# Staggered addresses for the gathered tokens and the SwiGLU product in an expert layer

## The chip, the cores and the metric

The kernel runs on one core of a Trainium2 chip, as one program. The metric is device time in microseconds (us). Before the change three runs took 1880.63, 1880.92 and 1881.67 us; the median is 1880.92 us.

## What is computed

The reference is a backbone of two layers over 256 latent tokens and 256 context tokens of width 1024. Layer 0 has attention and spatial gating, then a dense SwiGLU. Layer 1 has latent attention, and then the part that the change touches: each latent token goes to its two best of eight experts.

```python
def moe_swiglu(h, w_router, b_router, w_gate, w_up, w_down):
    ...
    y = jnp.zeros_like(h)
    for e in range(N_EXPERTS):                       # 8
        y = y + combine[..., e:e + 1] * swiglu(h, w_gate[e], w_up[e], w_down[e])
    return y

def swiglu(h, w_gate, w_up, w_down):                 # 1024 x 3584, 1024 x 3584, 3584 x 1024
    return (jax.nn.silu(h @ w_gate) * (h @ w_up)) @ w_down
```

All data are float32. The kernel gets float32 accuracy out of a faster multiplication by splitting both factors into a high and a low part and adding three products (high·high, high·low, low·high): the helper `mm3`, L213 to L216.

## The kernel before

**The stream of weights.** All weights come from memory in blocks of 128 x 2048 numbers (1 MB), in one fixed order, by transfers that SyncE issues (`load`, L157). Each block is split (`split`, L165): ScalarE writes the high part `wh` (L177), VectorE writes the low part `wl` (L178). There are three buffers of each. TensorE reads them, and when it is done with a buffer the next split may write it.

**The experts (L1129 to L1154).** For each of 8 experts `e` the tokens that chose it, at most 128, are gathered by matmuls into the tile `xg` (`gather`, L978): for each of 8 slices `k` of the width it holds a high and a low block of 128 x 128, so 16 blocks of 512 bytes in each partition. There are two buffers of `xg`; the gathering for expert `e + 1` is done in small steps during expert `e`. The hidden width is done in 7 chunks `c` of 512 columns. For each chunk:

- `expert_in` (L1027): gate and up. For each of 8 slices, three matmuls with a block of `xg` as the stationary operand (128 x 128) and 512 columns of `wh` or `wl` as the moving operand: 24 matmuls for the gate, 24 for the up, into the PSUM tiles `mm`. VectorE multiplies the two into the tile `a` (L1035).
- `turn` (L1038): four transposes of `a`, and a split of the result into the tiles `ahi` and `alo` (128 x 512 each, four blocks of 512 bytes in each partition; two buffers of each).
- `expert_out` (L1046): down. 24 matmuls with blocks of `ahi` and `alo` as stationary operand and 512 columns of `wh` or `wl` as moving operand, into the PSUM tiles `pss`. They accumulate over the 7 chunks.

The turn and the down matmuls of a chunk come inside and behind the gate and up of the next chunk. When an expert is done its result is put back to the tokens by eight matmuls that read the tiles `yh`, `yl` and `ST` (`scatter_steps`, L1084); the last expert uses `scatter_now` and the tile `a` instead.

**Order and queues.** Each engine has its own queue and does its instructions in order. The framework chooses the order within a queue by simulated readiness and puts in the waits. TensorE runs matmuls and the loads of the stationary operand (PEld in the profile) side by side: while one matmul streams, the block for the next is loaded.

**Where the tiles lie.** Tiles of 128 partitions lie at one byte address in every partition. In the program of before these are the addresses that matter:

| tile | address | address mod 256 |
|---|---|---|
| wh, three buffers | 52384, 60576, 68768 | 160 |
| wl, three buffers | 76960, 85152, 93344 | 160 |
| xg, two buffers | 138656, 146848 | 160 |
| ahi, two buffers | 185280, 187328 | 192 |
| alo, two buffers | 189376, 191424 | 192 |
| ah of layer 0 (L214 to L216, moving operand) | 109984, 118176 | 160 |
| hx of layer 0 at its start (stationary operand there) | 166432 and three more, 8192 apart | 32 |

Every moving operand of 512 columns starts a whole number of 2048 bytes from the start of its tile, and every stationary block a whole number of 512 bytes, so the last column holds for each matmul.

The gains of the final norm lie in the tile `fg` (128 x 1024), loaded by two transfers of ScalarE's queue (L1141 to L1143) and read by VectorE after the last expert (L1165, L1196).

Of the kernel before, what the change touches and what calls it, by code (L numbers as in the profile page):

```python
# [8 lines left out]
F32 = mybir.dt.float32  # L9
F32R = mybir.dt.float32r  # L10
I32 = mybir.dt.int32
AF = mybir.ActivationFunctionType
ALU = mybir.AluOpType
# [3 lines left out]
P = 128  # L17
KD = 8
# [94 lines left out]
def _program(tc, A, out):  # L113
    nc = tc.nc
    act, vec, pe = nc.scalar, nc.vector, nc.tensor

    def newpool(name, bufs, side="left"):
        return tc.alloc_tile_pool(name=name, bufs=bufs, side=side, reuse_waits="tile")
# [11 lines left out]
    def nm(s):  # L130
        uid[0] += 1
        return f"{s}{uid[0]}"

    def ps_mm():
        return psp.tile([P, 512], F32, tag="mm", name=nm("mm"), bufs=4)

    def ps_s():
        return psp.tile([P, 512], F32, tag="s", name=nm("pss"), bufs=2)

    def ps_t():  # L140
        return psp.tile([P, 512], F32, tag="t", name=nm("pst"), bufs=2)
# [76 lines left out]
    def put_split(hi, lo, src):  # L218
        return (act.activation(hi, src, AF.Copy),
                vec.tensor_tensor(lo, src, hi.bitcast(F32), ALU.subtract))  # L220

# [1 line left out]
    def cload(key, shape, pool=const):  # L223
        t = pool.tile(shape, F32, tag=key, name="c_" + key)
        nc.scalar.dma_start(t, A[key])
        return t

    x = xp.tile([P, KD, T], F32, tag="x", name="x")
# [69 lines left out]
    def filler(n, get_ps):  # L298
        for _ in range(n):
            ada_unit(get_ps)  # L300
# [24 lines left out]
    def stats_begin(nk, nt):  # L325
        return {"nk": nk, "nt": nt, "acc": None, "ps": None}
# [59 lines left out]
            vec.scalar_tensor_tensor(x[:, db, a:b], ps[:, a:b], mod[:, l, g0 + db, c:c + 1], x[:, db, a:b],  # L386
                                     ALU.mult, ALU.add)

# [1 line left out]
    st = stats_begin(KD, 4)  # L390
    for k in range(KD):
        stats_add(st, x[:, k, :], k)
# [151 lines left out]
    proj_tok(2, ev_v)  # L544
    gp.release()

# [1 line left out]
    atp = newpool("atp", 2)  # L548
    first_out = where["evo", 0, 1]
    mixah, mixal = hx_pair()  # L550
# [70 lines left out]
    make_a(0, 1)  # L621
    

# [1 line left out]
    st = stats_begin(KD, 4)  # L625
    for cb in range(2):
        pss = [ps_mm() for _ in range(4)]
# [14 lines left out]
    make_a(1, 0)  # L642
    filler(4, ps_mm)

# [1 line left out]
    ffp = newpool("ffp", 2)  # L646
    bc = stats_end(st, 1024)
    hh, hl = hx_pair(), hx_pair()
# [65 lines left out]
    ffp.release()  # L714
    hxp.release()

# [1 line left out]
    filler(4, ps_mm)  # L718
    mlp = newpool("mlp", 1)
    mrp = newpool("mrp", 1, "right")  # L720
# [128 lines left out]
    mop1 = newpool("mop1", 1)  # L849
    tri, iota, ltm = mc[:, 0:128], mc[:, 128:256], mc[:, 256:320]  # L850
    wr, br = mc[:, 320:384].rearrange("p (k e) -> p k e", e=8), mc[:, 384:392]
    acc = mop1.tile([P, 2, 1024], F32, tag="acc", name="acc")
# [14 lines left out]
    for cb in range(2):  # L867
        pss = [ps_mm() for _ in range(4)]
        for h in range(2):
            wh, wl = unit("mo", cb, h)  # L870
            for ct in range(4):
                for kk in range(4):
                    k = 4 * h + kk
# [15 lines left out]
        for tt in range(2):  # L889
# [3 lines left out]
            h_ = slice(512 * cb, 512 * cb + 512)  # L893
            put_split(hth[:, tt, h_], htl[:, tt, h_], pt)
    mohp.release()

    # x and the last gate by token
    for tt in range(2):
        for n in range(2):
            pt = ps_mm()  # L900
# [9 lines left out]
    def keep_clock(n, after=None):  # L910
        ps = ps_mm()
        with ExitStack() as es:
            if after is not None:
                es.enter_context(tc.issue_after(after.ins))
            for _ in range(n):
                pe.matmul(ps, lhsT=hth[:, 0, 0:P], rhs=hth[:, 0, 512:1024], start=True, stop=True)

    keep_clock(12)
# [1 line left out]
    mop = newpool("mop", 2)  # L920
    a_ = lg.unsqueeze(2).to_broadcast([P, 2, 8, 8])
    b_ = lg.unsqueeze(3).to_broadcast([P, 2, 8, 8])
# [28 lines left out]
    def slots(p_, e, tag="S", by=None):  # L951
        if by is None:
            s_ = mop.tile([P, 2 * P], F32R, tag=tag, name=nm(tag), bufs=1)
        else:
            s_ = mop.tile([P, 512], F32R, tag=tag, name=nm(tag), bufs=1)[:, 0:2 * P]
        for tt in range(2):
            o, at = s_[:, tt * P:tt * P + P], p_[:, tt, e:e + 1]
            if by is None:
                vec.tensor_scalar(o, iota, at, None, ALU.is_equal)
            else:  # L960
                vec.tensor_scalar(o, iota, at, by[:, tt:tt + 1], ALU.is_equal, ALU.mult)
        return s_
# [10 lines left out]
                put_split(h, l, t)  # L973
                yield

# [1 line left out]

    def gather(p_, e, raw=False):  # L978
        S = []
        xg = mop1.tile([P, KD, 2, P], F32R, tag="xg", name=nm("xg"), bufs=2)  # L980

        def steps():
            if raw:
                s_ = slots(p_, e, "yh", rsh.bitcast(F32))
                terms = [(hth, s_), (htl, s_), (hth, slots(p_, e, "yl", rsl))]
            else:
                S.append(slots(p_, e))
                terms = [(hth, S[0]), (htl, S[0])]
            yield
            for k in range(KD):  # L990
                pg = ps_mm() if front and k % 2 else ps_t()
                for i_, (hsrc, s_) in enumerate(terms):
                    for tt in range(2):
                        pe.matmul(pg[:, 0:P], lhsT=hsrc[:, tt, k * P:k * P + P], rhs=s_[:, tt * P:tt * P + P],
                                  start=(i_ == 0 and tt == 0), stop=(i_ == len(terms) - 1 and tt == 1))
                b = mod[:, 1, 24 + k, 0:1]
                hi, lo = xg[:, k, 0, :], xg[:, k, 1, :]
                ia = act.activation(hi, pg[:, 0:P], AF.Identity, bias=b)
                iv = vec.scalar_tensor_tensor(lo, pg[:, 0:P], b, hi.bitcast(F32), ALU.add, ALU.subtract)
                hold[:] = [ia, iv] if front else []  # L1000
                yield
            if raw:
                S.append(slots(p_, e))
        return xg, S, steps()
# [8 lines left out]
    def drain(g):  # L1013
        for _ in g:
            pass
# [11 lines left out]
    def expert_in(e, c, xg, mid, *tag):  # L1027
        pg = ps_mm()
        half(e, c, "mg", xg, pg, tag)
        a = mop.tile([P, 512], F32, tag="a", name=nm("a"))  # L1030
        act.activation(a, pg, AF.Silu)
        mid()
        pu = ps_mm()
        half(e, c, "mu", xg, pu, tag)
        vec.tensor_tensor(a, a, pu, ALU.mult)  # L1035
        return a

    def turn(stt):  # L1038
        pt = ps_t()
        for j in range(4):  # L1040
            pe.transpose(pt[:, j * P:j * P + P], stt["a"][:, j * P:j * P + P], ident)
        stt["hi"] = mop.tile([P, 512], F32R, tag="ahi", name=nm("ahi"))
        stt["lo"] = mop.tile([P, 512], F32R, tag="alo", name=nm("alo"))
        put_split(stt["hi"], stt["lo"], pt)

    def expert_out(e, c, stt, ys, *tag):  # L1046
# [47 lines left out]

    prev = None
    xg, S, g = gather(pos, 0, True)
    front.append(0)
    drain(g)
# [31 lines left out]
    for e in range(NE):  # L1130
        xg, S, g = nxt
        drain(g)
        for c in range(NCH):
            a = expert_in(e, c, xg, between)
            hold[:] = []
            if prev is not None:
                if prev["c"] == 0:
                    prev["ys"] = [ps_s(), ps_s()]
                finish()
            if e == NE - 1 and c == 3:  # L1140
                fg = mop1.tile([P, 2, 512], F32, tag="fg", name="fg")  # L1141
                for n in range(2):
                    nc.scalar.dma_start(fg[:, n, :], A["fg_row"][:, 512 * n:512 * n + 512])  # L1143
            if c == 2:
                ST = slots_T(S[0])
                if e < NE - 1:
                    nxt = gather(pos, e + 1, e == 0)
                    background.append(nxt[2])
                if e == 0:
                    background.append(normalize())  # L1150
            prev = {"e": e, "c": c, "a": a, "ST": ST, "ys": prev["ys"] if c else None}
# [6 lines left out]
    o = xrp.tile([P, 2, 1024], F32, tag="raw", name="fo")  # L1158
    halves = [(n, tt, slice(512 * n, 512 * n + 512)) for n in range(2) for tt in range(2)]

    def norm_parts():
        for n, tt, h_ in halves:
            act.activation(ps_t(), acc[:, tt, h_], AF.Square, accum_out=ss[:, tt, n:n + 1])
            if n == 0:
                vec.tensor_tensor(o[:, tt, h_], acc[:, tt, h_], fg[:, n, :], ALU.mult)  # L1165

    norm_parts()

    # experts with more tokens than one tile
    nmax = nc.values_load(cnt[0:1, 8:9], min_val=0, max_val=2 * P)  # L1170
    with tc.If(nmax > P):
        for e in range(NE):
            n_e = nc.values_load(cnt[0:1, e:e + 1], min_val=0, max_val=2 * P)
            with tc.If(n_e > P):
# [5 lines left out]
                for c in range(NCH):  # L1180
                    stt = {"a": expert_in(e, c, xo, lambda: None, "o")}
# [2 lines left out]
                scatter_now(e, ys, slots_T(so[0]))  # L1184
        norm_parts()

# [1 line left out]
    s2 = small([P, 2], tag="fs2", bufs=1)  # L1188
    vec.tensor_tensor(s2, ss[:, :, 0], ss[:, :, 1], ALU.add)  # L1189
    rs = rsqrt(s2, 2, 1.0 / 1024)  # L1190
    for n, tt, h_ in halves:
        r = rs[:, tt:tt + 1]
        if n == 0:
            act.activation(o[:, tt, h_], o[:, tt, h_], AF.Identity, scale=r)
        else:
            vec.scalar_tensor_tensor(o[:, tt, h_], acc[:, tt, h_], r, fg[:, n, :], ALU.mult, ALU.mult)  # L1196
        (nc.sync if n else nc.scalar).dma_start(out[0, tt * P:tt * P + P, h_], o[:, tt, h_])
    xrp.release()
    mop.release()
# [3 lines left out]
    return pools  # L1203


# [1 line left out]
def _layout(i):  # L1207
    f = np.float32
    A = {}
# [121 lines left out]
```

## Time and profile before

| | us |
|---|---|
| median of three runs | 1880.92 |
| span of the profiled execution, first to last instruction | 1880.0 |
| the three runs' own times | 1880.63 to 1881.67 |
| TensorE matmul busy | 1837.8 (98%) |
| weight loads (PEld) busy | 1438.2 (77%) |
| VectorE busy | 1331.9 (71%) |
| ScalarE busy | 1041.2 (55%) |

The profiled execution's own time is not listed apart from the runs; its span lies 0.6 to 1.7 us below the three times. In the profile, matmuls are pipelined: each shows some 390 ns, but the next one starts some 230 ns after it. So the cost of a matmul is read from the distance between starts in the timeline, not from its duration. DMA is the busy share of the core's 16 transfer engines.

### The profile page before, as it was taken

The page shows a single profiled execution, that of the slowest core. Times are in us where ns is not written, and L with a number is a line of the kernel's source. Part 1 is how long each engine was busy: PE and PEld are TensorE (multiplying, and loading weights), DVE is VectorE, ACT ScalarE, POOL GpSimd, SP SyncE. Part 2 cuts the span into 40 slices and gives each one's busy share as a digit, 9 for nine tenths or more (in the row PEclk, how much of TensorE's full clock was granted, in tenths as well). Part 3 has the DMA queues.
Part 4 walks back from the last instruction along what each step waited for, and adds up shares of the span by engine and source line. Part 5 has one row for each costly group of instructions (what it writes and reads, how often), then busy time and mean ns, then how long its engine had stood idle before and what let it go on. Part 6 is the DMA issues. An engine that isn't in the chain of part 4 may idle for free. (4 is left out here: it accounts for less than half of the span.)

```text
span 1880.0 us, 22323 instructions
## 1 busy us (share of the span) xinstructions
PE 1837.8 (98%) x8878; PEld 1438.2 (77%) x8878; DVE 1331.9 (71%) x1452; ACT 1041.2 (55%) x1082; POOL 0.2 (0%) x4
## 2 busy tenths in 40 slices
PE   6999999999999999999999999999999999999997
PEld 5775477878888877478788888887888888888885
DVE  5533655443434586568899889898898898988987
ACT  4223633222222244556777677777777777777774
POOL 0000000000000000000000000000000000000000
PEclk9999999999999999999999999999999999999998
DMA  9567233232222245367989999999999999999991
GB/s 369 191 221 273 99 116 123 97 139 90 90 90 101 98 135 168 114 242 284 357 335 358 339 353 363 335 356 358 341 351 347 356 350 339 360 360 345 356 362 47
DMA packets 68688, 475.05 MB, mean 253 GB/s; under 512 B 7520, under 2 KB 8160, under 8 KB 13024
## 3 DMA queue, kind: packets, MB, share of 16 engines
q1 hardware_dynamic: 66416, 469.27, 67.6%
q10 hardware_dynamic: 2160, 4.27, 0.6%
q8 instruction: 72, 1.18, 0.3%
q14 instruction: 40, 0.33, 0.0%
HBM read 470.36 MB, written 1.05 MB: 251 GB/s over the span
## 5 line engine op out<-in xcount | busy, mean ns | idle before, releaser
L178 DVE TENSOR_TENSOR wl<-raw,wh 128x2048 fp32r<-128x2048 f32 (+1 forms) x461 | 904.3, 1983 | 253.4 <-ACT wh L177 243.7
L177 ACT ACTIVATE wh<-raw 128x2048 fp32r<-128x2048 f32 (+1 forms) x461 | 763.8, 1670 | 360.7 <-PE mm L215 139.7
L214 PE MATMUL mm<-wh,xg 128*128 128x512 f32 x896 | 353.6, 395 | 0.0
L215 PE MATMUL mm<-wl,xg 128*128 128x512 f32 x896 | 352.3, 393 | 0.0
L216 PE MATMUL mm<-wh,xg 128*128 128x512 f32 x896 | 350.2, 391 | 0.0
L215 PEld LDWEIGHTS mm<-wl,xg 128*128 128x128 f32 x896 | 168.4, 188 | 35.0 <-DVE wl L178 1.6
L216 PEld LDWEIGHTS mm<-wh,xg 128*128 128x128 f32 x896 | 168.4, 188 | 34.4
L215 PE MATMUL mm<-hx,wh 128*128 128x512 f32 (+1 forms) x496 | 194.5, 392 | 0.1
L216 PE MATMUL mm<-hx,wl 128*128 128x512 f32 (+1 forms) x496 | 194.6, 393 | 0.0
L214 PEld LDWEIGHTS mm<-wh,xg 128*128 128x128 f32 x896 | 168.4, 188 | 34.2
L214 PE MATMUL mm<-hx,wh 128*128 128x512 f32 (+1 forms) x496 | 191.4, 394 | 3.0 <-ACT hx L377 3.0
L215 PE MATMUL pss<-wl,ahi 128*128 128x512 f32 x448 | 178.7, 399 | 0.6 <-DVE wl L178 0.6
L216 PE MATMUL pss<-wh,alo 128*128 128x512 f32 x448 | 177.0, 396 | 0.0
L214 PE MATMUL pss<-wh,ahi 128*128 128x512 f32 x448 | 170.7, 396 | 0.0
L214 PEld LDWEIGHTS mm<-hx,wh 128*128 128x128 f32 x496 | 93.7, 189 | 28.9 <-ACT hx L377 3.4
L215 PEld LDWEIGHTS mm<-hx,wh 128*128 128x128 f32 x496 | 94.0, 190 | 21.8 <-DVE hx L379 0.8
L216 PEld LDWEIGHTS mm<-hx,wl 128*128 128x128 f32 x496 | 93.9, 189 | 21.3
L215 PEld LDWEIGHTS pss<-wl,ahi 128*128 128x128 f32 x448 | 84.2, 188 | 21.9 <-DVE wl L178 2.9
L214 PEld LDWEIGHTS pss<-wh,ahi 128*128 128x128 f32 x448 | 84.2, 188 | 19.3
L216 PEld LDWEIGHTS pss<-wh,alo 128*128 128x128 f32 x448 | 84.2, 188 | 18.8
L386 DVE SCALAR_TENSOR_TENSOR x<-mm,mod,x 128x256 f32<-128x256 f32 x120 | 52.3, 478 | 51.1 <-PE mm L216 51.1
L214 PE MATMUL mm<-ah,wh 128*128 128x512 f32 x176 | 68.6, 391 | 0.2
(275 smaller groups left out, 1973.6 us busy)
## 6 DMA issues: line engine op xcount, KB each, us to landing
raw<-in_mg SPq DMA_DIRECT2D x112, 1024.0 KB, 7.0
raw<-in_mu SPq DMA_DIRECT2D x112, 1024.0 KB, 6.8
raw<-in_md SPq DMA_DIRECT2D x112, 1024.0 KB, 6.9
raw<-in_ada SPq DMA_DIRECT2D x48, 1024.0 KB, 5.7
raw<-in_na_in SPq DMA_DIRECT2D x10, 1024.0 KB, 5.3
raw<-in_fg SPq DMA_DIRECT2D x10, 1024.0 KB, 4.9
raw<-in_fu SPq DMA_DIRECT2D x10, 1024.0 KB, 4.9
raw<-in_fd SPq DMA_DIRECT2D x10, 1024.0 KB, 4.9
```

Of the source, the lines that this page charges most:

```text
L177: act.activation(h_, r_, AF.Copy)
L178: vec.tensor_tensor(l_, r_, h_.bitcast(F32), ALU.subtract)
L214: pe.matmul(ps, lhsT=lh, rhs=rh, start=start, stop=False)
L215: pe.matmul(ps, lhsT=lh, rhs=rl, start=False, stop=False)
L216: pe.matmul(ps, lhsT=ll, rhs=rh, start=False, stop=stop)
L386: vec.scalar_tensor_tensor(x[:, db, a:b], ps[:, a:b], mod[:, l, g0 + db, c:c + 1], x[:, db, a:b], ALU.mult, ALU.add)
```

## The change

The tile `xg` becomes flat and 64 numbers (256 bytes) longer, and expert `e` uses the part that begins `8 e` numbers (`32 e` bytes) in. The tiles `ahi` and `alo` become 256 bytes longer, and chunk `c` uses the part that begins `32 c` bytes in. To make room, the tile `fg` no longer has a place of its own: its two halves take the places of `yh` and `yl`.

```diff
     def gather(p_, e, raw=False):
         S = []
-        xg = mop1.tile([P, KD, 2, P], F32R, tag="xg", name=nm("xg"), bufs=2)
+        xg = mop1.tile([P, 2 * KD * P + 64], F32R, tag="xg", name=nm("xg"), bufs=2)
+        xg = xg[:, 8 * e:8 * e + 2 * KD * P].rearrange("p (k h s) -> p k h s", k=KD, h=2)
...
-        stt["hi"] = mop.tile([P, 512], F32R, tag="ahi", name=nm("ahi"))
-        stt["lo"] = mop.tile([P, 512], F32R, tag="alo", name=nm("alo"))
+        at = 8 * stt.get("c", 0)
+        stt["hi"] = mop.tile([P, 512 + 64], F32R, tag="ahi", name=nm("ahi"))[:, at:at + 512]
+        stt["lo"] = mop.tile([P, 512 + 64], F32R, tag="alo", name=nm("alo"))[:, at:at + 512]
         put_split(stt["hi"], stt["lo"], pt)
...
-                fg = mop1.tile([P, 2, 512], F32, tag="fg", name="fg")
+                fg = [mop.tile([P, 512], F32, tag=t, name=nm("fg"), bufs=1) for t in ("yh", "yl")]
                 for n in range(2):
-                    nc.scalar.dma_start(fg[:, n, :], A["fg_row"][:, 512 * n:512 * n + 512])
+                    nc.scalar.dma_start(fg[n], A["fg_row"][:, 512 * n:512 * n + 512])
```

The two readers of `fg` take `fg[n]` instead of `fg[:, n, :]`, and some comment lines are removed. No instruction is added or removed. Worked out from the tile sizes, the second buffer of `xg` moves up by 256 bytes, and the tiles of the pool that holds `yh`, `yl`, `a`, `ahi`, `alo` and `ST` move down by 3584 bytes or by other whole numbers of 256 bytes. So, apart from the staggering itself, every address keeps its value mod 256.

## Rows read from the trace of the kernel before

**Rows 1.** The costliest groups of the page: line, engine, operation, tiles, shapes, count | busy us, mean ns of one | idle time of the engine before them and what ended it.

```profile
L178 DVE TENSOR_TENSOR wl<-raw,wh 128x2048 fp32r<-128x2048 f32 (+1 forms) x461 | 904.3, 1983 | 253.4 <-ACT wh L177 243.7
L177 ACT ACTIVATE wh<-raw 128x2048 fp32r<-128x2048 f32 (+1 forms) x461 | 763.8, 1670 | 360.7 <-PE mm L215 139.7
L214 PE MATMUL mm<-wh,xg 128*128 128x512 f32 x896 | 353.6, 395 | 0.0
L215 PE MATMUL mm<-wl,xg 128*128 128x512 f32 x896 | 352.3, 393 | 0.0
L216 PE MATMUL mm<-wh,xg 128*128 128x512 f32 x896 | 350.2, 391 | 0.0
L215 PE MATMUL pss<-wl,ahi 128*128 128x512 f32 x448 | 178.7, 399 | 0.6 <-DVE wl L178 0.6
L216 PE MATMUL pss<-wh,alo 128*128 128x512 f32 x448 | 177.0, 396 | 0.0
L214 PE MATMUL pss<-wh,ahi 128*128 128x512 f32 x448 | 170.7, 396 | 0.0
```

**Rows 2.** Busy time by engine (count of instructions), granted TensorE clock as a share of full speed, DMA share and GB/s: the whole stage of the experts, and then one early and one late stretch of it.

```profile
862.70:1864.20 1001.50, 996.21 (x4571) 816.18 (x4571) 882.76 (x592) 723.45 (x531) 0.00 (x0) 1.00 0.92 341
...
1000.00:1100.00 100.00, 98.92 (x460) 81.27 (x459) 88.33 (x62) 71.86 (x56) 0.00 (x0) 1.00 0.93 350
...
1600.00:1700.00 100.00, 99.80 (x459) 81.56 (x458) 88.63 (x63) 72.10 (x55) 0.00 (x0) 1.00 0.96 356
```

**Rows 3.** Who waited for whom in the stage: the longest waits there (900 to 1850 us), and then all waits of TensorE's matmuls: total us, times, longest.

```profile
DVE wl L178 <- ACT wh L177: 81.2, 131, 1.1
ACT wh L177 <- PE mm L216: 80.7, 108, 1.8
ACT wh L177 <- PE pss L216: 67.9, 75, 1.3
...
PE pst L1041 <- DVE xg L999: 2.8, 4, 0.7
PE pst L994 <- DVE xg L999: 1.9, 5, 0.6
PE pss L215 <- DVE wl L178: 0.6, 3, 0.2
```

**Rows 4.** The timeline of TensorE (start us, duration us, engine, line, operation, tiles) through one gate of expert 1: the first seven matmuls, the last one (24 in all), and the matmul behind it.

```profile
1007.06 0.39 PE L214 MATMUL mm<-wh,xg 128*128 128x512 f32 x1
1007.29 0.40 PE L215 MATMUL mm<-wl,xg 128*128 128x512 f32 x1
1007.53 0.39 PE L216 MATMUL mm<-wh,xg 128*128 128x512 f32 x1
1007.75 0.40 PE L214 MATMUL mm<-wh,xg 128*128 128x512 f32 x1
1007.99 0.39 PE L215 MATMUL mm<-wl,xg 128*128 128x512 f32 x1
1008.22 0.39 PE L216 MATMUL mm<-wh,xg 128*128 128x512 f32 x1
1008.45 0.39 PE L214 MATMUL mm<-wh,xg 128*128 128x512 f32 x1
...
1012.30 0.40 PE L216 MATMUL mm<-wh,xg 128*128 128x512 f32 x1
1012.53 0.63 PE L214 MATMUL pss<-wh,ahi 128*128 128x512 f32 x2
```

**Rows 5.** The same view of one down product: the first and the last of its 24 matmuls.

```profile
1030.43 0.39 PE L214 MATMUL pss<-wh,ahi 128*128 128x512 f32 x1
...
1035.79 0.40 PE L216 MATMUL pss<-wh,alo 128*128 128x512 f32 x1
```

**Rows 6.** The same view in layer 0, with `hx` as the stationary operand: a first and a last matmul with 21 between them.

```profile
153.87 0.39 PE L215 MATMUL mm<-wl,hx 128*128 128x512 f32 x1
...
159.00 0.39 PE L216 MATMUL mm<-wh,hx 128*128 128x512 f32 x1
```

**Rows 7.** The same view in layer 0's SwiGLU, with `ah` as moving and `wh` as stationary operand: a first and a last matmul with 23 between them.

```profile
348.00 0.39 PE L214 MATMUL mm<-ah,wh 128*128 128x512 f32 x1
...
353.44 0.39 PE L214 MATMUL mm<-ah,wh 128*128 128x512 f32 x1
```

**Rows 8.** The tile `fg` (operation, count: duration ns min/median/max, first and last start us), the landing of its two transfers, the last reads of `yh` and `yl` before the tail, and ScalarE's timeline where the changed program's issue would come.

```profile
L1143 ACTq DMA_DIRECT2D fg<-in_fg_row x2: 334/394/455, 820.3 to 820.7; - x2
L1165 DVE TENSOR_TENSOR fo<-acc,fg x2: 681/686/692, 1866.0 to 1868.6; 128x512 f32<-128x512 f32 x2
...
DMA to landing us min/median/max: 8.5/9.9/11.3
...
L1076 PE MATMUL mm<-yl,ST x28: 389/393/396, 1006.4 to 1778.8; 128*128 128x512 f32 x28
...
1779.96 1.91 ACT L177 ACTIVATE wh<-raw 128x2048 fp32r<-128x2048 f32 x1
1782.22 1.92 ACT L177 ACTIVATE wh<-raw 128x2048 fp32r<-128x2048 f32 x1 [0.35 <-PE mm L216]
```

**Rows 9.** The instructions that write the moved tiles: shapes, count | busy us, mean ns.

```profile
L220 DVE TENSOR_TENSOR alo<-pst,ahi 128x512 fp32r<-128x512 f32 x56 | 38.2, 681 | 0.0
...
L219 ACT ACTIVATE ahi<-pst 128x512 fp32r<-128x512 f32 x56 | 33.4, 596 | 29.3 <-PE pst L1041 29.3
...
L998 ACT ACTIVATE xg<-pst,mod 128x128 fp32r<-128x128 f32 x60 | 21.6, 359 | 29.0 <-PE pst L994 29.0
L999 DVE SCALAR_TENSOR_TENSOR xg<-pst,mod,xg 128x128 fp32r<-128x128 f32 x60 | 20.7, 345 | 1.8 <-ACT xg L998 1.8
```

More of the change, by code (lines that the diff above doesn't have):

```diff
@@ L1164, in norm_parts @@
             if n == 0:
-                vec.tensor_tensor(o[:, tt, h_], acc[:, tt, h_], fg[:, n, :], ALU.mult)
+                vec.tensor_tensor(o[:, tt, h_], acc[:, tt, h_], fg[n], ALU.mult)
     norm_parts()
@@ L1195, in _program @@
         else:
-            vec.scalar_tensor_tensor(o[:, tt, h_], acc[:, tt, h_], r, fg[:, n, :], ALU.mult, ALU.mult)
+            vec.scalar_tensor_tensor(o[:, tt, h_], acc[:, tt, h_], r, fg[n], ALU.mult, ALU.mult)
         (nc.sync if n else nc.scalar).dma_start(out[0, tt * P:tt * P + P, h_], o[:, tt, h_])
```

## The prediction

> **What bounds the kernel now.** I began with the costliest groups: the 2688 gate and up matmuls (three lines of 896) and the 1344 down matmuls (three of 448) of the experts lead on TensorE, and nothing idles ahead of them [rows 1]. Then the windows: the experts run from 862.7 to 1864.2 us, 1001.5 us, with TensorE busy for 996.2 of them, VectorE for 882.8, ScalarE for 723.5, the granted clock at 1.00 (the 2.4 GHz level) and the DMA share at 0.92, up to 0.96 late in the stage [rows 2]. Then the waits, to see who is late: ScalarE's splits wait 148.6 us for TensorE to free a weight buffer, while TensorE's matmuls wait 5.3 us in the whole stage [rows 3]. So TensorE sets the pace, and the time of this stage is the number of matmuls times the distance between their starts. That distance is the subject of the change, for no instruction is added or removed.
>
> **The distance between starts depends on the two addresses.** All rows here are matmuls of 512 columns with a 128 x 128 stationary block; they differ in where the two operands lie. I call the stationary block's address minus the moving operand's address, mod 256, the offset (the table of addresses above has both). In the gate, `xg` (160) against `wh` or `wl` (160), the offset is 0: from 1008.22 to 1012.30 there are 18 steps, 4.08 us, 226.7 ns each; the first five steps of that gate, from 1007.06 to 1008.22, take 232 ns each, so the whole gate has 5.47 us for 24 steps, 227.9 ns [rows 4]. In the down product, `ahi` and `alo` (192) against 160, the offset is 32: 23 steps in 5.36 us, 233.0 ns, with no settling to anything shorter [rows 5]. `hx` (32) against 160 has offset 128: 22 steps in 5.13 us, 233.2 ns [rows 6]. `ah` as moving operand and `wh` as stationary one, both 160, again offset 0 with other tiles and roles: 24 steps in 5.44 us, 226.7 ns [rows 7]. So an offset of 0 settles to 226.7 ns, and both other offsets that I can see stay at 233. The difference follows the offset and not the tile.
>
> Here the Trainium skill would have it otherwise: "SBUF — State Buffer", section "Who interferes with whom", gives TensorE two independent read ports, one for the moving operand and one for the weights, and says that it never waits on anyone. By that, addresses would not matter and the change would cost nothing; rows 4 against rows 5 speak against it (226.7 against 233.0 ns), so it stands below as a rival only.
>
> **The change part by part.**
> - *`xg` staggered.* Expert 0 keeps offset 0, experts 1 to 7 get 32, 64, 96, 128, 160, 192 and 224. Each expert has 2688 / 8 = 336 gate and up matmuls [rows 1]. Offsets 32 and 128 are priced by rows 5 and 6: 233.0 - 227.9 = 5.1 ns more per matmul, so experts 1 and 4 cost 672 x 5.1 ns = 3.4 us. The other five experts, 1680 matmuls, have offsets that no row shows. Bounds: the shortest and the longest single step in the unsettled part of a gate, 0.22 us (1007.53 to 1007.75) and 0.24 us (1007.29 to 1007.53) [rows 4], give 1680 x (220 - 227.9) = -13.3 us and 1680 x (240 - 227.9) = +20.3 us. I take 233.0 ns, the value of both measured offsets other than 0: 1680 x 5.1 = 8.6 us. Together 12.0 us for 2352 matmuls.
> - *`ahi` and `alo` staggered.* They begin at offset 32, so chunk 0 keeps 32 and chunks 1 to 6 get 64, 96, 128, 160, 192 and 224: none gets 0. Offset 128 costs as much as 32. The five unseen ones have 5 x 24 x 8 = 960 matmuls; the same bounds give 960 x (220 - 233) = -12.5 us and 960 x (240 - 233) = +6.7 us, and at 233.0 ns the change is 0, which I take.
> - *`fg` in the places of `yh` and `yl`.* Its transfers left ScalarE's queue at 820 us and now have to wait for the last read of `yl`, at 1778.8 us; landing takes some 9.9 us, and the first reader comes at 1866.0 us, so some 77 us of slack hide it [rows 8]. Queued behind the waiting issue on ScalarE are the splits for TensorE (L177). At 1779.96 us a split starts and at 1782.22 us the next, after a wait for a buffer, so an issue of 0.4 us (two) has room [rows 8]. I take 0. Uncovered it would be the two issues and a wait of about one split, 0.8 + 1.9 = 2.7 us; a gain of 0.8 us at 820 us, where the two issues go from ScalarE's queue, is the other end.
> - *Writers of the moved tiles.* The splits and the gather's evacuations keep shape and count, 345 to 681 ns each [rows 9]. If an odd place cost them a tenth, that would be 11 us on two engines that have 119 and 278 us to spare [rows 2]; cost 0.
>
> *Sum.* 3.4 + 8.6 + 0 + 0 = +12.0 us on the span of 1880.0 us, 1892.0 us; the three runs lie 0.6 to 1.7 us above that span, the median 0.9, so 1892.9 us. Nothing hides the longer steps: the engine that grows is the one that the others wait for [rows 3], and 12 us more give the transfers more room, not less. What is late next does not arise.
>
> **Rivals.**
> - *A. The forecast*, all offsets other than 0 settle at about 233 ns: 1892.9 us. For it: two of two such offsets, over different tiles. Against it: five of seven are unseen.
> - *B. Some unseen offsets also settle at 226.7 ns.* Each one that does takes back 5.1 ns on 336 gate and up and 192 down matmuls, 2.7 us; two of five give 12.0 - 5.4 = +6.6 us, 1887.5 us; all five give -1.5 us, 1879.4 us. For it: nothing says that 0 alone is good. Against it: 32 and 128 do not, and they are an odd and an even multiple of the step.
> - *C. Addresses do nothing*, and the 6 ns belong to something else that goes with these tiles, such as the PSUM tile or the line. Time 1880.9 us. Against it: rows 5 and 6 write different PSUM tiles and agree, rows 4 and 6 write the same one and differ. The skill's rule above is this case.
> - *D. The other side: the unseen offsets are better than 0*, since the loading of the next block meets the moving stream at a better moment. It decides from a mean of 228.5 ns over the 2640 unseen matmuls, where 3.4 + 1680 (g - 227.9) + 960 (g - 233) is zero; at 224 ns it gives 3.4 - 6.6 - 8.6 = -11.8 us, 1869.1 us, and at 220 ns -22.4 us, 1858.5 us. For it: single steps of 0.22 us exist [rows 4]. Against it: they occur only in the unsettled part, each beside a longer one. The DMA share of 0.92 to 0.96 [rows 2] would let some 4% go before the transfers bound the stage.
> - *E. The unseen offsets are worse than 233 ns.* At 240 ns: 3.4 + 20.3 + 6.7 = +30.4 us, 1911.3 us; halfway, at 236.5 ns, 3.4 + 14.4 + 3.4 = +21.2 us, 1902.1 us.
>
> [...]
>
> **How the numbers follow.** A has 0.50, B 0.22, C 0.08, D 0.10, E 0.10. The time is A's, 1892.9 us. The range takes in A, C, nearly all of B, and the near part of E: 1880.5 to 1899 us; outside lie D and most of E, 0.18. A measurement of this kernel can tell 0.2%, about 3.8 us, from no change. Slower: A, E and B with up to three good offsets (0.17): 0.77. Same: C and B with four: 0.12. Faster: D and a little of B: 0.11.
>
> **What would show it.** In the changed trace the timeline of a gate of expert 0 should settle at 226.7 ns, those of experts 1 and 4 stay at 233 ns, and the other five tell A, B, D and E apart one by one, as chunks 1 to 6 do for the down product. The stage of the experts should be longer by 12 us with TensorE's waits as small as now, and nothing ahead of 862.7 us should move. `fg` should be issued after 1779 us and land long before its reader. I am wrong if the steps of experts 1 and 4 are at 227 ns (then it was not the offset), or if the stage grows by waits of TensorE instead of by its steps.

## The result, and the profile after

The changed kernel takes 1890.89 us, median of four runs (1890.52 to 1891.12), beside 1881.14 us for the kernel before: a ratio of 1.0052 with an interval of [1.0038, 1.0067]. It is 9.75 us or 0.5% slower, clear of the noise. The forecast was 1892.9 us. The profiled span is 1889.1 us, 9.1 us longer than the 1880.0 us of before. In every run behind the prediction whose span is listed, the run's time lies 1.7 to 2.0 us above that span, so the median of before, 1881.14 us, goes with a span of some 1879.3 us (an estimate): the profiled execution of before was some 0.7 us longer than its median, and 9.75 us is the better figure for the change.

The costliest groups of the page after, in the columns of [rows 1]:

```profile
L214 PE MATMUL mm<-wh,xg 128*128 128x512 f32 x896 | 357.1, 399 | 0.0
L215 PE MATMUL mm<-wl,xg 128*128 128x512 f32 x896 | 355.7, 397 | 0.0
L216 PE MATMUL mm<-wh,xg 128*128 128x512 f32 x896 | 353.4, 394 | 0.0
...
L215 PE MATMUL pss<-wl,ahi 128*128 128x512 f32 x448 | 178.8, 399 | 0.5 <-DVE wl L178 0.4
```

The counts are those of [rows 1]. The three lines with `xg` have grown by 3.2 to 3.5 us each, and TensorE idles before none of them; the down product has not moved. The windows, in the columns of [rows 2]: the stretch ahead of the experts, before and after the change, and then the stage of the experts after it, from the first gate matmul to the first matmul behind the last down product:

```profile
0.00:862.70 862.70, 838.06 (x4302) 620.78 (x4303) 441.35 (x842) 313.55 (x541) 0.20 (x4) 0.99 0.43 153
...
0.00:862.10 862.10, 837.32 (x4302) 620.73 (x4303) 441.51 (x842) 314.01 (x541) 0.20 (x4) 0.99 0.43 153
...
862.10:1873.20 1011.10, 1006.37 (x4571) 816.62 (x4570) 883.87 (x592) 724.24 (x531) 0.00 (x0) 1.00 0.91 338
```

The stage is 9.6 us longer than in [rows 2] (1011.1 against 1001.5), TensorE's busy time in it is 10.2 us longer, and the granted clock is the same. TensorE's waits there, as in [rows 3] (total us, times, longest), come to 4.6 us where they were 5.3:

```profile
PE pst L1042 <- DVE xg L1000: 2.6, 4, 0.7
PE pst L995 <- DVE xg L1000: 1.6, 5, 0.6
PE pss L215 <- DVE wl L178: 0.4, 2, 0.2
```

So the time came through the distance between starts. The timeline of TensorE shows it gate by gate. Here are the first and the last of the 24 matmuls (23 steps) of one gate of each expert, 0 to 7 in order, offsets 0, 32, 64 and so on to 224:

```profile
867.64 0.39 PE L214 MATMUL mm<-wh,xg 128*128 128x512 f32 x1
...
872.85 0.39 PE L216 MATMUL mm<-wh,xg 128*128 128x512 f32 x1
...
999.89 0.39 PE L214 MATMUL mm<-wh,xg 128*128 128x512 f32 x1
...
1005.25 0.40 PE L216 MATMUL mm<-wh,xg 128*128 128x512 f32 x1
...
1110.25 0.39 PE L214 MATMUL mm<-wh,xg 128*128 128x512 f32 x1
...
1115.62 0.39 PE L216 MATMUL mm<-wh,xg 128*128 128x512 f32 x1
...
1237.91 0.39 PE L214 MATMUL mm<-wh,xg 128*128 128x512 f32 x1
...
1243.30 0.39 PE L216 MATMUL mm<-wh,xg 128*128 128x512 f32 x1
...
1365.66 0.39 PE L214 MATMUL mm<-wh,xg 128*128 128x512 f32 x1
...
1371.02 0.40 PE L216 MATMUL mm<-wh,xg 128*128 128x512 f32 x1
...
1492.15 0.39 PE L214 MATMUL mm<-wh,xg 128*128 128x512 f32 x1
...
1497.52 0.39 PE L216 MATMUL mm<-wh,xg 128*128 128x512 f32 x1
...
1618.84 0.39 PE L214 MATMUL mm<-wh,xg 128*128 128x512 f32 x1
...
1624.10 0.39 PE L216 MATMUL mm<-wh,xg 128*128 128x512 f32 x1
...
1744.54 0.40 PE L214 MATMUL mm<-wh,xg 128*128 128x512 f32 x1
...
1749.91 0.40 PE L216 MATMUL mm<-wh,xg 128*128 128x512 f32 x1
```

Divide each difference by 23. Expert 0 has 5.21 us, 226.5 ns. Experts 1 to 5 have 5.36 to 5.39 us, 233 to 234 ns. Expert 6, at offset 192, has 5.26 us, 228.7 ns, nearly the short step. Expert 7 is back at 5.37 us, 233.5 ns. One gate is a sample, so I also took the mean over all steps between two matmuls of a kind, from the start times in the trace, leaving out steps above 245 ns (interrupted steps: there something else stands between the two starts). All later means "over all" are made so:

| offset | gate and up, ns | down, ns |
|---|---|---|
| 0 | 228.0 | none |
| 32 | 233.1 | 233.2 |
| 64 | 233.4 | 233.3 |
| 96 | 234.0 | 234.1 |
| 128 | 232.5 | 232.5 |
| 160 | 233.5 | 233.6 |
| 192 | 229.6 | 230 |
| 224 | 233.2 | 233.2 |

Counting in the step to whatever stands behind a product, if it is no longer than 245 ns, the gate and up step went from 228.02 to 232.15 ns over all experts. With some 2586 such steps in each kernel that is 10.7 us. The down steps came out 0.2 us shorter and the interrupted steps 0.8 us shorter, and the stage begins at 862.1 instead of 862.7 us. That is 10.7 - 0.2 - 0.8 - 0.6 = 9.1 us, the difference of the two spans. The 0.6 us need not be the change's: in the runs below whose program is the same up to the experts the stage begins anywhere between 860.6 and 863.2 us. Without it 9.7 us are left, beside 9.75 us between the medians.

### The profile page after: what moved, and what is told of

It reads as the page before. It is cut to its first block, busy times and chain, and to the rows that moved or that the text cites. A ratio compares the mean times of both kernels' runs of the same rounds, so it can differ in the third digit from the quotient of the medians.

```text
span 1889.1 us, 22321 instructions
## 1 busy us (share of the span) xinstructions
PE 1847.3 (98%) x8878; PEld 1438.7 (76%) x8878; DVE 1333.1 (71%) x1452; ACT 1042.4 (55%) x1082; POOL 0.2 (0%) x4
## 5 line engine op out<-in xcount | busy, mean ns | idle before, releaser
L214 PE MATMUL mm<-wh,xg 128*128 128x512 f32 x896 | 357.1, 399 | 0.0
L215 PE MATMUL mm<-wl,xg 128*128 128x512 f32 x896 | 355.7, 397 | 0.0
L216 PE MATMUL mm<-wh,xg 128*128 128x512 f32 x896 | 353.4, 394 | 0.0
L215 PEld LDWEIGHTS mm<-wl,xg 128*128 128x128 f32 x896 | 168.5, 188 | 38.1 <-DVE wl L178 1.4
L216 PEld LDWEIGHTS mm<-wh,xg 128*128 128x128 f32 x896 | 168.4, 188 | 37.8
L214 PEld LDWEIGHTS mm<-wh,xg 128*128 128x128 f32 x896 | 168.4, 188 | 37.3
L215 PE MATMUL mm<-hx,wh 128*128 128x512 f32 (+1 forms) x496 | 193.9, 391 | 0.1
L214 PE MATMUL mm<-hx,wh 128*128 128x512 f32 (+1 forms) x496 | 190.9, 393 | 3.0 <-ACT hx L377 3.0
L216 PE MATMUL mm<-hx,wl 128*128 128x512 f32 (+1 forms) x496 | 193.8, 391 | 0.0
L215 PE MATMUL pss<-wl,ahi 128*128 128x512 f32 x448 | 178.8, 399 | 0.5 <-DVE wl L178 0.4
L216 PE MATMUL pss<-wh,alo 128*128 128x512 f32 x448 | 176.7, 395 | 0.0
L214 PE MATMUL pss<-wh,ahi 128*128 128x512 f32 x448 | 170.6, 396 | 0.0
L214 PEld LDWEIGHTS mm<-hx,wh 128*128 128x128 f32 x496 | 93.6, 189 | 28.5 <-ACT hx L377 3.5
L215 PEld LDWEIGHTS mm<-hx,wh 128*128 128x128 f32 x496 | 93.7, 189 | 21.4 <-DVE hx L379 0.8
L216 PEld LDWEIGHTS mm<-hx,wl 128*128 128x128 f32 x496 | 93.5, 189 | 21.0
L215 PEld LDWEIGHTS pss<-wl,ahi 128*128 128x128 f32 x448 | 84.3, 188 | 20.9 <-DVE wl L178 2.5
L214 PEld LDWEIGHTS pss<-wh,ahi 128*128 128x128 f32 x448 | 84.2, 188 | 19.6
L216 PEld LDWEIGHTS pss<-wh,alo 128*128 128x128 f32 x448 | 84.3, 188 | 18.8
L214 PE MATMUL mm<-ah,wh 128*128 128x512 f32 x176 | 68.7, 391 | 0.2
```

The lines of the kernel that those rows point to most:

```text
L214: pe.matmul(ps, lhsT=lh, rhs=rh, start=start, stop=False)
L215: pe.matmul(ps, lhsT=lh, rhs=rl, start=False, stop=False)
L216: pe.matmul(ps, lhsT=ll, rhs=rh, start=False, stop=stop)
```

## The experiments

Each edit is shown against the changed kernel, and all runs keep its longer tiles and the moved `fg`. The ratio is that to the kernel before, timed beside it.

**No stagger, only the room for it.**

```diff
-        xg = xg[:, 8 * e:8 * e + 2 * KD * P].rearrange("p (k h s) -> p k h s", k=KD, h=2)
+        xg = xg[:, 0:0 + 2 * KD * P].rearrange("p (k h s) -> p k h s", k=KD, h=2)
...
-        at = 8 * stt.get("c", 0)
+        at = 0
```

> The longer tiles and the move of fg stay, the staggering is taken out: tokens at offset 0, product at offset 32, as before the change. Offset theory (the step between matmuls depends on the stationary address minus the moving address, mod 256): steps of a gate 228 ns and of a down product 233 ns, time as before, 1881 us, or 0.6 us less because fg no longer loads ahead of the experts. Rival, place and form (the longer flat tiles or the moved fg cost the time): about 1891 us.

Measured: 1881.36 us beside 1881.15, ratio 1.0002 [0.9992, 1.0012]. Over all, the gate and up step is 227.8 ns and the down step 232.9. The longer tiles, the flat form and the move of `fg` cost nothing that shows; the whole difference belongs to the stagger. The run also shows that offsets 256 bytes apart are alike: the two buffers of `xg`, used in turn, now lie 33 x 256 bytes apart, and the even experts have 228.0 ns, the odd ones 227.7.

**The tokens alone.**

```diff
-        at = 8 * stt.get("c", 0)
+        at = 0
```

> Only the gathered tokens are staggered, the product stays at offset 32. Offset theory: the steps by expert are those of the changed kernel (228.0 at offset 0; 233.1 to 234.0 at 32, 64, 96, 160, 224; 232.5 at 128; 229.6 at 192), 336 of each: +11 us on the gate and up, so 1890 to 1892 us, the whole of the change. Rival, shared cost (the staggered product carries part of it): 1885 to 1888 us.

Measured: 1892.38 us, ratio 1.0061 [1.0044, 1.0078], 0.4 us above the expected range. The steps by expert are those of the table, 229.5 ns at offset 192 among them. This half carries the whole cost.

**The product alone.**

```diff
-        xg = xg[:, 8 * e:8 * e + 2 * KD * P].rearrange("p (k h s) -> p k h s", k=KD, h=2)
+        xg = xg[:, 0:0 + 2 * KD * P].rearrange("p (k h s) -> p k h s", k=KD, h=2)
```

> Only the SwiGLU product is staggered, the tokens stay at offset 0. Offset theory: down steps 233 to 234 ns at all offsets but 192, and 230 there, 192 matmuls of 1344: 0 to -0.6 us, so 1880 to 1881 us. Rival, shared cost: 1884 to 1887 us.

Measured: 1880.34 us, ratio 0.9996 [0.9986, 1.0005]. Chunk 5, at offset 192, has 229.1 ns per step, the others stay near 233. So the product's stagger gains on 192 matmuls some 192 x 4 ns = 0.8 us, too little to be timed. The two halves do not touch each other: the sum of their differences, 11.2 - 0.8 = 10.4 us, agrees with the 9.75 us of the whole change within the intervals.

**Tokens at 0, product at 0 too.** If the offset sets the step, the down product, which before the change never had offset 0, must become shorter when it gets it.

```diff
-        xg = xg[:, 8 * e:8 * e + 2 * KD * P].rearrange("p (k h s) -> p k h s", k=KD, h=2)
+        xg = xg[:, 0:0 + 2 * KD * P].rearrange("p (k h s) -> p k h s", k=KD, h=2)
...
-        at = 8 * stt.get("c", 0)
+        at = 56
```

> Tokens at offset 0 for every expert and the product moved to offset 0 for every chunk (224 bytes further than at the start of its tile). Offset theory: the down steps fall from 233 to about 228 ns, 1344 x 5.1 = 6.9 us, so 1873.5 to 1875 us. Rival, tile theory (the down product is slow for another reason that goes with its tiles, such as its PSUM tiles): 1881 us and steps of 233 ns.

Measured: 1873.51 us, ratio 0.9957 [0.9940, 0.9973], faster than both kernels. The first and last matmul of one down product in TensorE's timeline, and then the window of the stage:

```profile
976.47 0.39 PE L214 MATMUL pss<-wh,ahi 128*128 128x512 f32 x1
...
981.68 0.39 PE L216 MATMUL pss<-wh,alo 128*128 128x512 f32 x1
```

```profile
862.20:1856.40 994.20, 988.80 (x4572) 815.66 (x4571) 882.80 (x592) 723.69 (x531) 0.00 (x0) 1.00 0.92 344
```

The 23 steps take 5.21 us, 226.5 ns, where [rows 5] had 5.36 us for the same 23 (over all 227.5 ns). The stage is 7.3 us shorter than in [rows 2] (994.2 against 1001.5) with the same work, and the 1344 down matmuls give 1344 x (233 - 227.5) = 7.4 us.

**The other operand moved.** Nothing is staggered; the weight buffers `wh` and `wl`, the moving operand, lie 32 bytes further, and what lies behind them a whole 256 bytes further. The gate's offset becomes 224 and the down product's 0, with `xg`, `ahi` and `alo` at the same addresses mod 256 as before the change.

```diff
-    acol = const.tile([P, 4, KD, 2], F32, tag="acol", name="acol")
+    acol = const.tile([P, 8 * KD + 8], F32, tag="acol", name="acol")[:, 0:8 * KD].rearrange("p (a k c) -> p a k c", a=4, c=2)
...
-        xg = xg[:, 8 * e:8 * e + 2 * KD * P].rearrange("p (k h s) -> p k h s", k=KD, h=2)
+        xg = xg[:, 0:0 + 2 * KD * P].rearrange("p (k h s) -> p k h s", k=KD, h=2)
...
-        at = 8 * stt.get("c", 0)
+        at = 0
...
-    s2 = small([P, 2], tag="fs2", bufs=1)
+    s2 = small([P, 58], tag="fs2", bufs=1)[:, 0:2]
```

> No staggering; instead the weight buffers wh and wl, the moving operands, lie 32 bytes further, and everything allocated behind them 256 bytes further, so that the addresses of the stationary tiles keep their value mod 256. The offsets become 224 for gate and up, 0 for down, 32 for layer 0's ah against wh, 160 and 96 for hx. Offset theory (the difference of the two addresses counts): gate steps 233 ns (+5.2 x 2688 = 14.0 us), down steps 228 ns (-5.1 x 1344 = -6.9 us), ah against wh 233 ns (+5.1 x 620 = 3.2 us), hx as before: +10 us, 1891 us. Rival, own address (what counts is where the stationary block itself lies, mod 256): gate 228 and down 233 ns as before, 1881 us.

Measured: 1894.57 us, ratio 1.0069 [1.0050, 1.0088]. TensorE's timeline through one gate and one down product, the first and last matmul of each:

```profile
1007.33 0.39 PE L214 MATMUL mm<-wh,xg 128*128 128x512 f32 x1
...
1012.69 0.40 PE L216 MATMUL mm<-wh,xg 128*128 128x512 f32 x1
...
1019.89 0.39 PE L214 MATMUL pss<-wh,ahi 128*128 128x512 f32 x1
...
1025.11 0.40 PE L216 MATMUL pss<-wh,alo 128*128 128x512 f32 x1
```

The two have changed places: 5.36 us, 233.0 ns in the gate (over all 233.3), and 5.22 us, 227.0 ns in the down product (over all 227.7). Neither `xg` nor `ahi` has another place mod 256, so it is the distance between the operands that decides and not where the stationary one lies; nor is it where `wh` and `wl` lie, since with one place of theirs, before as here, one product is short and the other long. The time is 3.6 us above the 1891 us expected. The rest of the loss lies ahead of the experts, whose stage begins at 868.9 us and not at 862.1. The 528 products of [rows 7]'s kind went from offset 0 to 32, and from 227.0 to 233.2 ns over all: 3.3 us, as expected. Not expected were the 96 products with `mixbh` and `mixbl` as moving operand, which also left offset 0 (227.0 to 233.3 ns, 0.6 us), and the change of `hx` from offset 128 to 160 (moving, 1416 matmuls, 233.1 to 233.4 ns) and 96 (stationary, 288 matmuls, 232.7 to 234.2 ns), another 0.9 us.

**Every expert at offset 32.**

```diff
-        xg = xg[:, 8 * e:8 * e + 2 * KD * P].rearrange("p (k h s) -> p k h s", k=KD, h=2)
+        xg = xg[:, 8:8 + 2 * KD * P].rearrange("p (k h s) -> p k h s", k=KD, h=2)
...
-        at = 8 * stt.get("c", 0)
+        at = 0
```

> The tokens of every expert lie 32 bytes further, the product not at all: offset 32 for all 4032 matmuls of the experts. Offset theory: gate and up steps 233.1 ns everywhere, 2688 x 5.1 = 13.7 us, less up to 1 us that TensorE's few waits give back: 1893 to 1895 us. Rival, variety (it is the change of offset from expert to expert that costs, not its value): 1881 us.

Measured: 1894.10 us, ratio 1.0075 [1.0058, 1.0092]; over all 233.1 ns in the gate and up products. The window of the stage:

```profile
860.60:1874.50 1013.90, 1009.36 (x4571) 816.72 (x4571) 883.97 (x592) 723.38 (x531) 0.00 (x0) 1.00 0.91 337
```

That the offset differs from expert to expert is not what costs: one offset for all, 32, costs a little more than the stagger, since the stagger leaves expert 0 at 0 and gives expert 6 offset 192.

**Everything at offset 192.**

```diff
-        xg = xg[:, 8 * e:8 * e + 2 * KD * P].rearrange("p (k h s) -> p k h s", k=KD, h=2)
+        xg = xg[:, 48:48 + 2 * KD * P].rearrange("p (k h s) -> p k h s", k=KD, h=2)
...
-        at = 8 * stt.get("c", 0)
+        at = 40
```

> Tokens and product all at offset 192, the only other offset at which the changed kernel had short steps. Offset theory: gate and up 229.6 ns (+1.6 x 2688 = 4.3 us), down 230 ns (-3.0 x 1344 = -4.0 us): within 1 us of before, 1880 to 1882 us. Rival (192 was short by chance of when those experts and chunks came): 233 ns in both, 1893 to 1895 us.

Measured: 1878.82 us, ratio 0.9990 [0.9980, 0.9999], 1.2 us below the expected range. One gate of expert 1, first and last matmul:

```profile
998.15 0.39 PE L214 MATMUL mm<-wh,xg 128*128 128x512 f32 x1
...
1003.41 0.39 PE L216 MATMUL mm<-wh,xg 128*128 128x512 f32 x1
```

5.26 us for 23 steps, 228.7 ns, the same as expert 6 of the changed kernel; over all 229.3 in the gate and up products and 229.2 in the down product. So the good step of expert 6 was the offset's and not that expert's. What the down product gains by 192 (3.8 ns) more than pays for what the gate loses (1.3 ns on twice the matmuls): 5.1 against 3.5 us.

**The low blocks 128 bytes away from the high ones.** Each product runs in threes: L214 has the high block, L215 the high block again with other weights, L216 the low block. With high at offset 0 and low at 128, the three steps differ in which block is streamed against and which is loaded for the next matmul.

```diff
-        xg = xg[:, 8 * e:8 * e + 2 * KD * P].rearrange("p (k h s) -> p k h s", k=KD, h=2)
+        xg = [xg[:, a:a + KD * P].rearrange("p (k s) -> p k s", k=KD) for a in (0, KD * P + 32)]
...
-                hi, lo = xg[:, k, 0, :], xg[:, k, 1, :]
+                hi, lo = xg[0][:, k, :], xg[1][:, k, :]
...
-                mm3(ps, xg[:, k, 0, :], xg[:, k, 1, :], wh[:, 512 * kk:512 * kk + 512],
+                mm3(ps, xg[0][:, k, :], xg[1][:, k, :], wh[:, 512 * kk:512 * kk + 512],
...
-        at = 8 * stt.get("c", 0)
+        at = 0
```

> The low blocks of the tokens lie 128 bytes further than the high ones: of each three matmuls two have a stationary block at offset 0 and the third at 128; the product stays at 32. If the collision is between the moving stream and the loading of the next block, the step from the second to the third matmul of a triple, during which the low block is loaded, is the long one; if it is a matmul's own block, the step after the third. Either way one or two of three steps grow: +3 to +9 us each third (896 x 3 to 10 ns), 1884 to 1890 us. If one step out of its place keeps all three from settling, all are near 233 ns: 1894 us.

Measured: 1889.17 us, ratio 1.0047 [1.0030, 1.0063]. A stretch of TensorE's timeline in a gate:

```profile
1002.95 0.40 PE L216 MATMUL mm<-wh,xg 128*128 128x512 f32 x1
1003.18 0.39 PE L214 MATMUL mm<-wh,xg 128*128 128x512 f32 x1
1003.41 0.40 PE L215 MATMUL mm<-wl,xg 128*128 128x512 f32 x1
1003.64 0.40 PE L216 MATMUL mm<-wh,xg 128*128 128x512 f32 x1
1003.88 0.39 PE L214 MATMUL mm<-wh,xg 128*128 128x512 f32 x1
1004.10 0.40 PE L215 MATMUL mm<-wl,xg 128*128 128x512 f32 x1
1004.34 0.40 PE L216 MATMUL mm<-wh,xg 128*128 128x512 f32 x1
```

From each L216 to the next there are 0.69 to 0.70 us, three steps of 230 to 233 ns. Over all, the step behind L214 takes 228.2 ns, behind L215, while the low block is loaded, 232.3, and behind L216, while the low block is in use, 233.1. This does not tell the two apart: were it only the block being loaded, the step behind L216 would be short, were it only the block in use, the one behind L215. Either both count, or what one step loses shows in the next as well. It stays open.

**Offset 0 in layer 0 too.** The run with both expert products at 0, and one constant tile 128 bytes longer, which moves `hx` and the split tiles of the latent attention to offset 0. In most of these products `hx` is the moving operand and `wh` or `wl` the stationary one (1416 matmuls of 512 columns in the trace, against 288 with `hx` stationary as in [rows 6]); offset 128 becomes 0 in both.

```diff
-    ones = wp.tile([P, P], F32, tag="ones", name="ones")
+    ones = wp.tile([P, P + 32], F32, tag="ones", name="ones")[:, 0:P]
...
-        xg = xg[:, 8 * e:8 * e + 2 * KD * P].rearrange("p (k h s) -> p k h s", k=KD, h=2)
+        xg = xg[:, 0:0 + 2 * KD * P].rearrange("p (k h s) -> p k h s", k=KD, h=2)
...
-        at = 8 * stt.get("c", 0)
+        at = 56
```

> The tokens and the product at offset 0 as in e4_zero, and 128 bytes more in the tile ones, which lies above hx and the latent attention's split tiles on the same side, so that all of these also come to offset 0 against wh and wl. Offset theory: some 1700 matmuls of 512 columns with hx fall from 233 to about 228 ns, 1700 x 5.1 = 8.7 us, where TensorE is the bound; layer 0 has more waits than the experts, so 4 to 9 us below e4_zero: 1864.5 to 1869.5 us. Rival (layer 0 is bound by the splits or the transfers, and TensorE's gain is given back in waits): within 2 us of e4_zero, 1872 to 1874 us, with short steps all the same.

Measured: 1864.07 us beside 1880.94, ratio 0.9912 [0.9896, 0.9929]: 16.9 us less than the kernel before, the best of all versions here. One product with `hx` as the moving operand, first and last matmul, and then the windows before and in the stage of the experts:

```profile
244.55 0.39 PE L214 MATMUL mm<-hx,wh 128*128 128x512 f32 x1
...
249.76 0.39 PE L216 MATMUL mm<-hx,wl 128*128 128x512 f32 x1
```

```profile
0.00:850.80 850.80, 826.53 (x4302) 619.94 (x4302) 441.22 (x841) 313.50 (x541) 0.20 (x4) 0.99 0.44 155
...
850.80:1845.00 994.20, 988.83 (x4572) 815.84 (x4571) 882.76 (x592) 723.51 (x531) 0.00 (x0) 1.00 0.92 344
```

5.21 us for 23 steps, 226.5 ns. Over all, `hx` moving has 227.1 ns where the run with the expert products alone at 0 has 232.9, and `hx` stationary 227.7 where that has 232.3: 1416 x 5.8 + 288 x 4.6 ns = 9.5 us. By the medians the two runs lie 9.4 us apart, 0.4 us more than expected, so nothing of it is given back in waits. In the traces the experts begin 11.4 us earlier (850.8 against 862.2 us), of which some 2 us lie within what that moment varies from run to run; their stage is the same 994.2 us.

**Offsets that are no multiple of 32.** `xg` at 16 bytes, the product at 8.

```diff
-        xg = xg[:, 8 * e:8 * e + 2 * KD * P].rearrange("p (k h s) -> p k h s", k=KD, h=2)
+        xg = xg[:, 4:4 + 2 * KD * P].rearrange("p (k h s) -> p k h s", k=KD, h=2)
...
-        at = 8 * stt.get("c", 0)
+        at = 58
```

> How exact the offset must be: no staggering, tokens at offset 16, product at offset 8. If the memory is read in pieces of 32 bytes or more and the offset counts in such pieces, both are as offset 0: gate and up 228 ns, down 228 ns, 1873 to 1875 us. If every byte counts: gate and up about 233 ns (+13.7 us), down 233 ns (0), 1893 to 1895 us. Mixed, where 8 bytes are near enough and 16 are not: 1886 to 1888 us.

Measured: 1886.70 us, ratio 1.0036 [1.0022, 1.0050]. One gate, first and last matmul, and then another one from its second matmul to its last:

```profile
1126.19 0.40 PE L214 MATMUL mm<-wh,xg 128*128 128x512 f32 x1
...
1131.56 0.39 PE L216 MATMUL mm<-wh,xg 128*128 128x512 f32 x1
```

```profile
954.60 0.39 PE L215 MATMUL mm<-wl,xg 128*128 128x512 f32 x1
...
959.59 0.39 PE L216 MATMUL mm<-wh,xg 128*128 128x512 f32 x1
```

The first gate has 5.37 us for 23 steps, 233.5 ns; the second has 4.99 us for 22, 226.8 ns. Both are at offset 16. Over all, the step is 231.9 ns at offset 16 and 230.7 at offset 8, but only the second is a step of its own: all 56 down products at offset 8 average 230 to 231 ns. At offset 16 the mean is a mix of two kinds. Of 112 gate and up products 18 average 226.6 to 226.9 ns, as at offset 0, 80 average 233 to 233.6 ns, as at offset 32, and the 14 between change from one to the other on the way, mostly behind an interrupted step. So operands in the same 32 bytes mod 256 are not safe. The time falls into the range of the mixed case, but not for its reason, since neither offset behaves like 0 throughout.

## Why the prediction was right

*What bounds the kernel.* Right. TensorE's waits did not grow (4.6 us), no other engine came near (VectorE, the next, was busy for 883.9 of 1011.1 us), and the longer steps went into the span nearly one for one, as the shorter ones did in the runs with offset 0.

*The offset as the cause.* Right, and now shown from both sides: the step follows the offset when the stationary operand moves (tokens alone, product at 0) and when the moving one does. Rival C, that addresses do nothing, falls by the same runs. If the two independent read ports that the Trainium skill gives TensorE ("SBUF — State Buffer", section "Who interferes with whom") are taken to mean that addresses cost no time, this case does not agree: 226.5 against 233.5 ns at the same clock with the same work, in the gates of experts 0 and 7 above. Whether it is the ports that the two streams meet at, no run here shows.

*`xg` staggered, 2352 x 5.1 ns = 12.0 us.* Mis-sized: it measured 10.7 us. The step of experts 1 and 4 was right (233.1 and 232.5 ns where 233.0 was taken). The part that failed is "I take 233.0 ns, the value of both measured offsets other than 0" for all five unseen ones: four of them do have 233.2 to 234.0, but 192 has 229.6. Expert 6 so costs 336 x 1.6 = 0.5 us instead of 1.7, which is 1.2 us of the difference. The other six average 233.3, which gives back some 0.4 to 0.6 us, and on the 103 interrupted steps the stagger costs nothing, 0.5 us less. Rival B, some unseen offsets good, came true for one of five, and for that one only in part. That the other four are like 32 and 128 was taken from two rows and not known; the prediction gave it 0.50.

*`ahi` and `alo` staggered, 0.* Right within 0.2 us: the six chunks that moved keep 233 ns but for chunk 5, again at 192.

*`fg`, 0.* Right. The tile's rows after the change, as in [rows 8], and ScalarE's timeline around the two issues:

```profile
L1145 ACTq DMA_DIRECT2D fg<-in_fg_row x2: 335/348/361, 1787.6 to 1788.0; - x2
L1167 DVE TENSOR_TENSOR fo<-acc,fg x2: 686/689/692, 1875.0 to 1877.6; 128x512 f32<-128x512 f32 x2
...
DMA to landing us min/median/max: 2.6/2.9/3.2
```

```profile
1787.55 0.34 ACTq L1145 DMA_DIRECT2D fg<-in_fg_row  x1
1787.99 1.92 ACT L177 ACTIVATE wh<-raw 128x2048 fp32r<-128x2048 f32 x1
1788.01 0.36 ACTq L1145 DMA_DIRECT2D fg<-in_fg_row  x1
1790.11 1.92 ACT L177 ACTIVATE wh<-raw 128x2048 fp32r<-128x2048 f32 x1 [0.20 <-PE mm L216]
```

The issues come at 1787.6 us and land within 3.2 us, 84 us ahead of the first reader. A split starts between the two, and the one behind still waits for a buffer. The 0.8 us at the other end, named as a possible gain, is not shown: the 0.6 us by which the stage begins earlier are less than that moment varies from run to run, and the run with only the room for the stagger, which holds this gain too, does not time as faster.

*The sum, +12.0 us.* The steps of `xg` 10.7, those of the product -0.2, and the interrupted steps -0.8, which had no term of their own in the prediction: 9.7 us, beside the 9.75 us between the medians. Why the interrupted steps became shorter, no run here shows.

*Rivals D and E.* Neither. None of the offsets tried is better than 0, and the worst, 96, has 234.0 ns, where E wanted 236.5 or more.

## What to carry to other kernels

Where 128 x 128 blocks in fp32r are loaded for matmuls of 512 columns one behind the other, place the stationary operand and the moving operand at the same address mod 256: here that is worth 6.5 ns in each 233 where the steps have settled, some 5 to 6 ns over all, and 16.9 us of 1881 when all products get it. Compute the offset from the allocation and read the step from the starts in the timeline; a busy share of 98% on TensorE says nothing about it. A stagger, or a small tile put ahead of large ones, can change the offset of everything behind it.

## What the runs showed that I had not expected

- The offset acts in steps that settle into short cycles. By the differences of starts in the trace, offset 0 repeats 226, 227, 227 ns, 192 repeats 226, 229, 232 (mean 229), 32 swings between 231 or 232 and 235, and 128 between 229 and 238. The means alone hide that.
- The loss is no matter of equal or not equal: 0, 8, 16 and 32 bytes have 227.5 to 228.0, 230.7, 231.9 (a mix of 226.7 and 233) and 233.1 ns, and 192 has 229 while 160 and 224 on either side of it have 233.5 and 233.2.
- At offset 0 a gate sometimes begins with a few steps of about 232 ns before it settles, as in [rows 4], which is why its mean over all is 227.5 to 228 and not 226.7.
- At offset 16 the same product is short in one place and long in another, so at some offsets the address alone does not settle the step. What decides there was not tried.
- Why 256 bytes is the period, and what the two operands meet at, no run here shows.
